# High and low parts of transposed weight operands, side by side instead of one after the other

## The chip, the core and the metric

The kernel runs on one core of a Trainium2 chip. The metric is the device time of one execution in microseconds. Before the change it is 2574.55 us, the median of three runs (2573.84 to 2575.4).

## What is computed

A decoder trunk of two layers on 256 tokens of width 2048, in float32. Each layer has one input projection for four groups of heads (retention, stick-breaking attention, a gated linear recurrence, sparse attention), an output projection, cross-attention into 256 memory tokens, and a gated feed-forward part of width 5632 with a causal convolution of width 3. Cut to the products that matter here:

```
for layer in range(DEPTH):
    proj = rms_norm(x, mix_norm[layer]) @ w_in[layer]
    ...
    mix = jnp.concatenate([o.reshape(B, S, GROUP_WIDTH) for o in (o_ret, o_sb, o_hg, o_nsa)], axis=-1)
    x = x + mix @ w_out[layer]
    x = x + cross_attention(...)            # ends in (o @ wo)
    x = x + conv_ffn(...)                   # ends in (silu(gate) * val) @ w_down
return rms_norm(x, final_norm)
```

## The kernel before, in words

Every float32 matrix product is made of products of parts. A float32 operand v is split into a high part, rounded to the type that the rows call fp32r, and a low part, v minus the high part, of the same type. A product is hi x hi + hi x lo + lo x hi.

The weight matrices come from HBM in **units** of up to 128 x 1024 numbers, in an order fixed by `plan()`. TensorE (PE) multiplies; for each unit SyncE (SP) issues a DMA into `raw`, ScalarE (ACT) writes the high part `hi` (L422), and VectorE (DVE) writes the low part `lo` (L250, called by `u_lo`). These run some units ahead of PE (`AHEAD`, `HI`, `LO`). There are two kinds of units:

- `group_b` (L506, L509): the result is wanted transposed, with features on the partitions. The unit's `hi` and `lo` are the stationary operand (the weights that a load puts into the array) and the activations `xt` stream past: 512 columns at L506 (high and low part of 256 tokens in one go), 256 at L509.
- `group_a` (`mm_a`, L437 to L439): the result is wanted with tokens on the partitions. Here the transposed activations are the stationary operand, 128 tokens at a time, and the unit's `hi` and `lo` stream past, mostly 512 columns. For each block of 128 features and each half of the tokens there are three matmuls: high part against `hi` (L437), high part against `lo` (L438), low part against `hi` (L439). `group_tail` (L473 to L475) does the same for the last chunk of the last down projection, with the second half of the tokens in two pieces of 256 columns each.

In the rows a matmul's operands read out<-moving,stationary, in alphabetical order: acc<-hi,mg at L437 streams `hi` past `mg`.

The transposed activations are tiles of 128 partitions x 2 x 256: high part of 256 tokens, then low part. They have two tags with 16 buffers each. Tiles named `xt` come from the norms; the input projection and the up projection use them on both sides. Tiles named `mg` are, first, the results of the four mixers (made in `to_mix`, `stick`, and `item` in `nsa`), of cross-attention (`xout`) and of the gated feed-forward part (`ev_up`), which are only ever weights, in the output projection, `xattn_wo` and the down projection; and second, the normed memory tokens, which are used on both sides, at L506 and L509 among others and, as weights, for products of 256 columns at L437 to L439. The helper `hi_part` writes the high part on ACT (L245 or L263), `lo_part` the low part on DVE (L250 or L253), from the value and the high part just written.

A weight load is an instruction of its own on PE (PEld in the rows); PE runs it while the matmul before it is still streaming. The order of instructions on each engine is that in which the program is written out: a loop over the units with generators (`tick`) that put the other work between them. Each engine works in its order, and semaphores hold it where operands aren't ready.

Of the kernel before, what the change touches and what calls it, by code (L numbers as in the profile page):

```python
# [10 lines left out]
F32R = mybir.dt.float32r  # L11
# [183 lines left out]
def body(ctx, tc, w, x, xt_in, mem, mem_t, pos, consts, masks, pars, wck, wcv, fnorm, out):  # L195
    nc = tc.nc
    AHEAD, HI, LO = 6, 3, 2
    off, _, _ = shape_consts()
# [3 lines left out]
    flow = ctx.enter_context(tc.tile_pool(name="flow", bufs=1))  # L202
# [7 lines left out]
    def nm(p):  # L210
        count[0] += 1
        return f"{p}{count[0]}"
# [12 lines left out]

    def xt_tile(tag):
        return flow.tile([128, 2, 256], F32R, name=nm(tag), tag=tag, bufs=16)

    def f(ap):
        return ap.bitcast(F32)  # L230
# [443 lines left out]
    def layer(l):  # L674
# [118 lines left out]
        def to_mix(y, heads, base, gname):  # L793

            ps = yield from bank([128, 2, 256])
            for q in range(2):
                for t in range(2):
                    T.transpose(ps[:, q, t * 128:(t + 1) * 128], y[:, t, q, :], ident)
            yield
            o = [xt_tile("mg") for _ in range(2)]  # L800
            for q in range(2):
                hi_part(o[q], ps[:, q, :], pc(l, gname, heads[q]))
            yield
            for q in range(2):
                lo_part(o[q], ps[:, q, :], pc(l, gname, heads[q]))
                mix[base + heads[q]] = o[q]
            drop()
# [158 lines left out]
        def stick(h):  # L966
            yield from need("sq", "sk")
            qh, kh = W["sq"][h // 2][:, h % 2, :], W["sk"][h // 2][:, h % 2, :]
            ps = yield from bank([128, 3, 128])
            pf = ps.rearrange("p a b -> p (a b)")  # L970
            T.matmul(pf[:, 0:256], lhsT=kh[:, 0:128], rhs=qh, start=True, stop=True)
            T.matmul(pf[:, 256:384], lhsT=kh[:, 128:256], rhs=qh[:, 128:256], start=True, stop=True)
            if h == H - 1:
                W.pop("sq")
                W.pop("sk")
            qh = kh = None
            yield
            z, e = s_tile([128, 3, 128]), s_tile([128, 3, 128])
            A.copy(z[:, 1, :], ps[:, 1, :])
            tt(z[:, 0::2, :], ps[:, 0::2, :], bc(c("sbm"), 2), OP.add)  # L980
            drop()
            yield
            act(e, z, AF.Abs)
            act(e, e, AF.Exp, scale=-1.0)
            act(e, e, AF.Ln, bias=1.0)
            yield
            stt(e, z, 0.0, e, OP.max, OP.add)
            yield
            ef = e.rearrange("p a b -> p (a b)")
            ps = yield from bank([128, 384])  # L990
            T.matmul(ps[:, 0:256], lhsT=c("tri"), rhs=ef[:, 0:256], start=True, stop=False)
            T.matmul(ps[:, 128:256], lhsT=c("ones"), rhs=ef[:, 256:384], start=False, stop=False)
            T.matmul(ps[:, 256:384], lhsT=c("tri"), rhs=ef[:, 256:384], start=False, stop=True)
            e = ef = None
            yield
            zf = z.rearrange("p a b -> p (a b)")
            tt(zf, zf, ps, OP.subtract)
            drop()
            yield
            act(zf, zf, AF.Exp)  # L1000
            yield
            yield from need("sv")
            v = W["sv"]
            po = yield from bank([128, 256])
            T.matmul(po, lhsT=v[0][:, cols(h)], rhs=zf[:, 0:256], start=True, stop=False)
            T.matmul(po[:, 128:256], lhsT=v[1][:, cols(h)], rhs=zf[:, 256:384], start=False, stop=True)
            z = zf = v = None
            if h == H - 1:
                W.pop("sv")
            yield  # L1010
            o = xt_tile("mg")
            hi_part(o, po)
            yield
            lo_part(o, po)
            drop()
            mix[4 + h] = o


        def nsa():
            yield from need("nq")  # L1020
            qT = []
            for p in range(2):
                o = yield from to_feat(W["nq"], (2 * p, 2 * p + 1))
# [18 lines left out]
            for i, pn in enumerate(("pk", "pv")):  # L1042
                wn = s_tile([128, 32, 15])
                a = kv[:, i, :].rearrange("p (a b) -> p b a", b=16)
                for u in range(2):
                    o = PC[pn] + 16 * u
# [76 lines left out]
            def item(h, t):  # L1123
                wd = 128 * (t + 1)
                ps = yield from bank([128, 2, wd])
                T.matmul(ps, lhsT=qT[h // 2][:, h % 2, t * 128:(t + 1) * 128], rhs=kT[:, :, 0:wd],
                         start=True, stop=True)
                yield
                p = s_tile([128, 2, wd])
                stt(p, ps, SCALE, bc(c("cm", 256 - wd, 256), 2), OP.mult, OP.add)  # L1130
                drop()
                mx, sm, cf = small(2), small(2), small(2)
                V.tensor_reduce(mx, p, axis=AX.X, op=OP.max)
                ts(mx, mx, -1.0, None, OP.mult)
                yield
                for b in range(2):
                    act(p[:, b, :], p[:, b, :], AF.Exp, bias=mx[:, b:b + 1], accum=sm[:, b:b + 1])
                yield
                ts(sm, sm, 1e-30, None, OP.max)
                V.reciprocal(cf, sm)  # L1140
                tt(cf, cf, gate[t][:, 3 * h + 1:3 * h + 3], OP.mult)
                for b in range(2):
                    ts(p[:, b, :], p[:, b, :], cf[:, b:b + 1], None, OP.mult)
                yield
                ps = yield from bank([128, 2, t + 1, 128])
                for b in range(2):
                    for k in range(t + 1):
                        T.transpose(ps[:, b, k, :], p[:, b, k * 128:(k + 1) * 128], ident)
                p = None
                yield  # L1150
                pT = s_tile([128, 2, t + 1, 128])
                A.copy(pT, ps)
                drop()
                yield
                if t == 0:
                    pos_[h] = yield from bank([128, 256])
                po = pos_[h]
                o = po[:, t * 128:(t + 1) * 128]
                T.matmul(o, lhsT=vc[0:15, :], rhs=pcT[t][0:15, h, :], start=t == 0, stop=False)
                for b in range(2):  # L1160
                    for k in range(t + 1):
                        T.matmul(o, lhsT=nv[:, k, b, :], rhs=pT[:, b, k, :], start=False,
                                 stop=t == 1 and b == 1 and k == t)
                pT = None
                if t == 1:
                    yield
                    o = xt_tile("mg")
                    hi_part(o, pos_[h])
                    yield
                    lo_part(o, pos_.pop(h))  # L1170
                    drop()
                    mix[12 + h] = o
# [216 lines left out]
        def xout(h):  # L1389
            while h not in X["p"]:  # L1390
                yield
            po = yield from bank([128, 256])
            for m in range(2):
                T.matmul(po, lhsT=X["v"][h // 2][:, m, (h % 2) * 128:(h % 2 + 1) * 128], rhs=X["p"][h][:, m, :],
                         start=m == 0, stop=m == 1)
            X["p"][h] = None
            yield
            o = xt_tile("mg")
            hi_part(o, po)
            yield  # L1400
            lo_part(o, po)
            drop()
            xo[h] = o
# [18 lines left out]
        def ev_up(g):  # L1422
            def ev(ps):
                u = yield from whole(ps)
                yield from known(nf)
                tt(u, u, bc(nf.rb, 2), OP.mult)
                yield
                o = s_tile([128, 2, 256])
                for q in range(2):
                    ft = q * FT + g  # L1430
                    act(o[:, q, :], u[:, q, :], AF.Identity, scale=pc(l, "cw", 4 * FT + ft), bias=pc(l, "cb", ft))
                yield
                for q in range(2):
                    ft = q * FT + g
                    stt(o[:, q, 1:256], u[:, q, 0:255], pc(l, "cw", 2 * FT + ft), o[:, q, 1:256], OP.mult, OP.add)
                    stt(o[:, q, 2:256], u[:, q, 0:254], pc(l, "cw", ft), o[:, q, 2:256], OP.mult, OP.add)
                yield
                act(o[:, 0, :], o[:, 0, :], AF.Silu)
                yield
                tt(o[:, 0, :], o[:, 0, :], o[:, 1, :], OP.mult)  # L1440
                yield
                x_ = xt_tile("mg")
                hi_part(x_, o[:, 0, :])
                yield
                lo_part(x_, o[:, 0, :])
                gts[g] = x_
            return ev
# [247 lines left out]
```

## Time and profile before

| | |
|---|---|
| median of 3 runs | 2574.55 us (2573.84 to 2575.4) |
| the profiled execution, its own time | 2574.59 us |
| its span, first to last instruction | 2572.8 us |
| PE busy | 99% |
| PEld busy (weight loads, beside PE) | 85% |
| DVE busy | 69% |
| ACT busy | 53% |
| granted TensorE clock, mean | 0.999 of full |

Busy time of PE is counted from the start of a matmul to its end, and matmuls overlap, so its share is close to 100% wherever they follow without a gap. What a matmul costs in a row of them is read from the distance of two starts. The span is shorter than the execution by what lies ahead of the first instruction and behind the last.

### The profile page before, as it was taken

Reading aid. Unit: us, or ns where it says so; the run is one execution under the profiler, and the core shown is the slowest. Engines: PE = TensorE matmul, PEld = TensorE weight load, DVE = VectorE, ACT = ScalarE, POOL = GpSimd, SP = SyncE. Lnnn points to the kernel's source line nnn. Section 1 sums busy time; section 2 is a strip of 40 time slices with the busy share of each in tenths; the row PEclk is TensorE's granted clock in tenths of the full one; section 3 lists DMA queues with packets and bytes.
Section 4 is the critical chain, followed back from the end, with each engine's and each line's share of the span. In section 5 each row is a group of like instructions: output and inputs, shape, how many; then the busy total and the mean of one; then the engine's idle time right before and its main releaser. Section 6 shows DMA issues by size and latency. Waiting matters only on the chain. (4 is left out here: it accounts for less than half of the span.)

```text
span 2572.8 us, 37308 instructions
## 1 busy us (share of the span) xinstructions
PE 2554.7 (99%) x13866; PEld 2197.5 (85%) x13866; DVE 1777.8 (69%) x2881; ACT 1364.3 (53%) x2158; POOL 45.4 (2%) x79
## 2 busy tenths in 40 slices
PE   9999999999999999999999999999999999999998
PEld 7888888888888888888889888889888888888887
DVE  7776666667767676676767666656686777766766
ACT  6545545565555555455555455445664545454554
POOL 0010000000000000000000100000000000000000
PEclk9999999999999999999999999999999999999999
DMA  8574466545556555556555744655455555556654
GB/s 286 174 231 140 151 202 221 185 149 191 195 190 196 189 195 190 193 187 195 188 183 161 228 134 155 204 182 185 154 193 192 192 192 193 192 190 193 210 190 147
DMA packets 136582, 483.66 MB, mean 188 GB/s; under 512 B 15952, under 2 KB 16464, under 8 KB 136400
## 3 DMA queue, kind: packets, MB, share of 16 engines
q1 hardware_dynamic: 131024, 464.75, 55.0%
q0 software_dynamic: 4800, 15.73, 1.9%
q8 instruction: 109, 1.79, 0.3%
q10 hardware_dynamic: 576, 0.79, 0.1%
q14 instruction: 73, 0.60, 0.1%
HBM read 479.12 MB, written 2.10 MB: 187 GB/s over the span
## 5 line engine op out<-in xcount | busy, mean ns | idle before, releaser
L250 DVE TENSOR_TENSOR lo<-raw,hi 128x1024 fp32r<-128x1024 f32 (+3 forms) x881 | 1066.8, 1212 | 723.8 <-PE acc L438 255.7
L422 ACT CAST hi<-raw 128x1024 fp32r<-128x1024 f32 (+2 forms) x879 | 916.7, 1044 | 1132.1 <-PE acc L439 486.1
L506 PE MATMUL acc<-xt,hi 128*128 128x512 f32 x3456 | 868.8, 394 | 6.1 <-ACT hi L1599 6.1
L506 PEld LDWEIGHTS acc<-xt,hi 128*128 128x128 f32 x3456 | 619.7, 188 | 118.1 <-ACT hi L1599 6.1
L509 PEld LDWEIGHTS acc<-xt,lo 128*128 128x128 f32 x3456 | 460.0, 188 | 36.9
L509 PE MATMUL acc<-xt,lo 128*128 128x256 f32 x3456 | 465.7, 277 | 0.0
L437 PE MATMUL acc<-hi,mg 128*128 128x512 f32 (+1 forms) x1136 | 433.2, 381 | 0.2
L439 PE MATMUL acc<-hi,mg 128*128 128x512 f32 (+1 forms) x1136 | 428.8, 377 | 0.0
L438 PE MATMUL acc<-lo,mg 128*128 128x512 f32 (+1 forms) x1136 | 428.6, 377 | 0.0
L437 PE MATMUL acc<-hi,xt 128*128 128x512 f32 (+2 forms) x640 | 252.1, 394 | 0.0
L439 PEld LDWEIGHTS acc<-hi,mg 128*128 128x128 f32 x1136 | 213.7, 188 | 39.9 <-DVE mg L250 0.3
L437 PEld LDWEIGHTS acc<-hi,mg 128*128 128x128 f32 x1136 | 213.8, 188 | 39.4 <-ACT mg L263 1.0
L438 PEld LDWEIGHTS acc<-lo,mg 128*128 128x128 f32 x1136 | 213.8, 188 | 38.4
L439 PE MATMUL acc<-hi,xt 128*128 128x512 f32 (+2 forms) x640 | 243.1, 380 | 0.0
L438 PE MATMUL acc<-lo,xt 128*128 128x512 f32 (+2 forms) x640 | 242.9, 379 | 0.0
L253 DVE SCALAR_TENSOR_TENSOR s<-s,par,s 128x255 f32<-128x255 f32 x352 | 161.9, 481 | 6.3
L438 PEld LDWEIGHTS acc<-lo,xt 128*128 128x128 f32 x640 | 120.4, 188 | 20.8 <-issue 1.9
L437 PEld LDWEIGHTS acc<-hi,xt 128*128 128x128 f32 x640 | 120.3, 188 | 20.9 <-issue 2.3
L439 PEld LDWEIGHTS acc<-hi,xt 128*128 128x128 f32 x640 | 120.1, 188 | 20.6
L245 ACT ACTIVATE s<-s,par 128x256 f32<-128x256 f32 x176 | 96.1, 594 | 0.4 <-DVE s L250 0.4
L250 DVE TENSOR_TENSOR s<-acc,s 128x256 f32<-128x256 f32 x224 | 83.8, 416 | 0.3 <-ACT s L520 0.3
L250 DVE TENSOR_TENSOR x<-x,acc 128x512 f32<-128x512 f32 x128 | 81.5, 677 | 1.5 <-PE acc L475 1.5
(202 smaller groups left out, 1420.1 us busy)
## 6 DMA issues: line engine op xcount, KB each, us to landing
raw<-in_w_dram SPq DMA_DIRECT2D x847, 512.0 KB, 3.4
raw<-in_w_dram SPq DMA_DIRECT2D x16, 396.0 KB, 3.1
raw<-in_w_dram SPq DMA_DIRECT2D x16, 384.0 KB, 3.0
s<-in_nsa_w_ck_dram POOLq DMA_DIRECT2D x16, 256.0 KB, 5.5
s<-in_nsa_w_cv_dram POOLq DMA_DIRECT2D x16, 256.0 KB, 4.6
s<-in_memt_dram POOLq DMA_DIRECT2D x16, 256.0 KB, 5.3
s<-in_xt_dram SPq DMA_DIRECT2D x8, 256.0 KB, 6.5
x<-in_x_dram SPq DMA_DIRECT2D x8, 256.0 KB, 7.6
```

The costliest lines, as they stand in the source:

```text
L245: A.activation(o, i, func, bias=bias, scale=scale)
L250: V.tensor_tensor(o, a, b, op=op)
L253: V.scalar_tensor_tensor(o, a, s, b, op0=op0, op1=op1)
L422: A.copy(u.hi[:, a:b], u.raw[:, a:b])
L437: T.matmul(ps[t][:, 0:n], lhsT=xh, rhs=hi, start=first, stop=False)
L438: T.matmul(ps[t][:, 0:n], lhsT=xh, rhs=lo, start=False, stop=False)
L439: T.matmul(ps[t][:, 0:n], lhsT=xl, rhs=hi, start=False, stop=last)
L506: T.matmul(st["ps"][q].rearrange("p a b -> p (a b)"), lhsT=u.hi[:, at:at + 128], rhs=xk[kk].rearrange("p a b -> p (a b)"), start=i == 0 an ...
L509: T.matmul(st["ps"][q][:, 1, :], lhsT=u.lo[:, at:at + 128], rhs=xk[kk][:, 0, :], start=False, stop=i == 3 and kk == 3)
```

## The change

A second helper beside `xt_tile` makes a tile of the same size and tag in which the high and the low part of each element lie side by side: 128 partitions x 256 x 2. It gives back a view with the two axes swapped, so that the code which indexes the tile stays as it is: `o[:, 0, :]` is the high part, now with a step of two elements, and `o[:, 1, :]` the low part. The five places which make tiles that serve only as weights call it. The memory tiles, also tagged `mg`, and all `xt` tiles keep the old layout. The order of the instructions on each engine is what it was. Line numbers behind L229 grow by five.

```diff
+    def paired():
+
+        o = flow.tile([128, 256, 2], F32R, name=nm("mg"), tag="mg", bufs=16)
+        return o.rearrange("p a b -> p b a")
+
...
-            o = [xt_tile("mg") for _ in range(2)]
+            o = [paired() for _ in range(2)]
             for q in range(2):
                 hi_part(o[q], ps[:, q, :], pc(l, gname, heads[q]))
...
-            o = xt_tile("mg")
+            o = paired()
             hi_part(o, po)
             yield
             lo_part(o, po)
...
-                    o = xt_tile("mg")
+                    o = paired()
                     hi_part(o, pos_[h])
...
-            o = xt_tile("mg")
+            o = paired()
             hi_part(o, po)
...
-                x_ = xt_tile("mg")
+                x_ = paired()
                 hi_part(x_, o[:, 0, :])
```

## Rows read from the trace of the kernel before

**Rows 1.** The page's first part: busy time, share of the span, instructions.

```profile
PE 2554.7 (99%) x13866; PEld 2197.5 (85%) x13866; DVE 1777.8 (69%) x2881; ACT 1364.3 (53%) x2158; POOL 45.4 (2%) x79
```

**Rows 2.** Waits of PE: who for whom, us in total, times, longest us.

```profile
PE acc L506 <- ACT hi L1599: 6.1, 1, 6.1
PE wk L1394 <- ACT s L1383: 1.3, 2, 0.7
...
```

**Rows 3.** Busy time by stretch, down projection: stretch, us, engines, clock, DMA share, GB/s.

```profile
680.00:710.00 30.00, 30.00 (x134) 24.86 (x133) 19.72 (x25) 12.35 (x14) 0.00 (x0) 1.00 0.59 197
```

**Rows 4.** Timeline of PE in that stretch: start us, length us, what.

```profile
689.92 0.39 PE L439 MATMUL acc<-hi,mg 128*128 128x512 f32 x1
...
690.60 0.39 PE L439 MATMUL acc<-hi,mg 128*128 128x512 f32 x1
```

**Rows 5.** Timeline of PE at the kernel's end, matmuls of 256 columns.

```profile
2560.16 0.28 PE L473 MATMUL acc<-hi,mg 128*128 128x256 f32 x1
...
2560.64 0.28 PE L474 MATMUL acc<-lo,mg 128*128 128x256 f32 x1
```

**Rows 6.** Timeline of PE around a pause after a group.

```profile
1496.40 0.39 PE L438 MATMUL acc<-lo,xt 128*128 128x512 f32 x1
1496.63 0.39 PE L439 MATMUL acc<-hi,xt 128*128 128x512 f32 x1
1497.52 0.60 PE L1114 MATMUL wk<-cst,s 128*15 128x128 f32 x4 [0.50 <-DVE s L250]
```

**Rows 7.** Timeline of the weight loads (PEld) in the same stretch.

```profile
1496.41 0.19 PEld L439 LDWEIGHTS acc<-hi,xt 128*128 128x128 f32 x1
1497.49 0.34 PEld L1114 LDWEIGHTS wk<-cst,s 128*15 128x15 f32 x4 [0.90 <-ACT s L245]
```

**Rows 8.** Timeline of PE where it waited for the last mg tile.

```profile
2536.84 0.39 PE L439 MATMUL acc<-hi,mg 128*128 128x512 f32 x1
2537.31 0.50 PE L437 MATMUL acc<-hi,mg 128*128 128x512 f32 x1
2537.65 0.40 PE L438 MATMUL acc<-lo,mg 128*128 128x512 f32 x1
```

**Rows 9.** Groups by line and form: count, busy us, mean ns, idle before.

```profile
L437 PE MATMUL acc<-hi,mg 128*128 128x512 f32 x1008 | 395.3, 392 | 0.2
L437 PEld LDWEIGHTS acc<-hi,mg 128*128 128x128 f32 x1136 | 213.8, 188 | 39.4 <-ACT mg L263 1.0
L473 PE MATMUL acc<-hi,mg 128*128 128x512 f32 x8 | 3.1, 392 | 0.0
L473 PE MATMUL acc<-hi,mg 128*128 128x256 f32 x8 | 2.3, 282 | 0.0
```

**Rows 10.** Timeline of DVE at the start of `decays`.

```profile
76.47 0.28 DVE L844 COPY s<-s 128x256 f32<-128x256 f32 x1
76.78 0.42 DVE L250 TENSOR_TENSOR s<-s 128x256 f32<-128x256 f32 x1
```

**Rows 11.** Groups by line and form: writers of mg tiles, and one other on ACT.

```profile
L263 ACT CAST mg<-s 128x256 fp32r<-128x256 f32 x88 | 35.0, 398 | 0.0
L263 ACT CAST mg<-wk 128x256 fp32r<-128x256 f32 x24 | 8.5, 369 | 3.7 <-PE wk L1394 2.6 <-PE wk L1162 1.1
L245 ACT ACTIVATE mg<-wk,par 128x256 fp32r<-128x256 f32 x16 | 6.7, 466 | 0.0
L245 ACT ACTIVATE de<-s 128x256 f32<-128x256 f32 x32 | 11.6, 409 | 1.6 <-DVE s L250 1.5
L250 DVE TENSOR_TENSOR mg<-s,mg 128x256 fp32r<-128x256 f32 x88 | 36.9, 419 | 0.7 <-ACT mg L263 0.7
```

**Rows 12.** Timeline of PE in the up projection, merged rows.

```profile
1001.33 1.07 PE L509 MATMUL acc<-xt,lo 128*128 128x256 f32 x8
1002.24 2.00 PE L506 MATMUL acc<-xt,hi 128*128 128x512 f32 x8
1004.08 1.07 PE L509 MATMUL acc<-xt,lo 128*128 128x256 f32 x8
```

## The prediction

> **What bounds the kernel now.** I read the shares of the engines first. TensorE (PE) is busy 2554.7 of 2572.8 us; VectorE (DVE) has 69%, ScalarE (ACT) 53% [rows 1]. Then I asked what PE waits for: the view of waits has five rows for it, the longest 6.1 us before the first matmul, the next 1.3, so at most 6.1 + 4 x 1.3 = 11 us [rows 2]. A stretch of the down projection, 680 to 710 us, shows the same from close by: PE busy 30.00 of 30.00 us at a granted clock of 1.00, weight loads (PEld) 24.86, DVE 19.72, ACT 12.35 [rows 3]. So only what changes the beat of the matmuls changes the time; work on ACT and DVE has cover.
>
> The length that a row gives for a matmul (0.39 us) is not its beat, since matmuls overlap. The beat is the distance of their starts. In the down projection it is 690.60 - 689.92 = 0.68 us for three, 0.227 each for 512 columns [rows 4]. At the end of the kernel the same three lines run with 256 columns: 2560.64 - 2560.16 = 0.48 us for four, 0.120 each [rows 5]. The difference, 0.107 us for 256 columns, is 2.4 columns per ns, the upper clock level. So a matmul of this kind costs columns / 2.4 GHz plus a **fixed part**: 0.227 - 0.213 = 0.0135 us, and 0.120 - 0.107 = 0.0133. That fixed part is the only thing in these stretches that a different weight layout could give back, and the question is what it is.
>
> The rows say that it is not the next weight load disturbing the running matmul. At 1496.63 an L439 matmul of 512 columns starts and takes 0.39 us; the next weight load starts only at 1497.49, when it is over [rows 6, 7]. The matmuls before it take the same 0.39 with a load beside them. A load that reads SBUF in another way can't save what is there without any load. The load itself is short: where PE had waited for the mg tile, the matmul's length includes its own load, 0.50 instead of 0.39, so 0.11 us [rows 8], against a beat of 0.227.
>
> **The change part by part.** No instruction is added, removed or moved; the order on PE, DVE and ACT is the same, waits included, and so are the sizes of all buffers. What changes are steps: 8 bytes instead of 4 between elements of the tiles that `paired` makes, in the reads of weight loads, in the writes of the high part (ACT), and in the read and writes of the low part (DVE).
>
> *Weight loads, 512 columns.* L437, L438 and L439 have 1008 matmuls of 512 columns each with mg weights, and lines 473 to 475 have 8 each in the last chunk (for each of the two trios one row is shown) [rows 9]. Together 3 x 1016 = 3048, and 3048 x 0.227 = 691 us of the time. Each load (0.11 us) lies under the matmul before it (0.227) and has 0.117 us to spare. No row shows a weight load with a step, so its cost is bounded from both sides. From below: 0, by the same step in another reader: the DVE copy at L844 and the addition behind it read and write with step two, and the addition takes 0.42 us [rows 10], as the unstepped mg<-s,mg does (419 ns) [rows 11]. From above: twice the time, 0.22 us, which is still under 0.227. I take 0, since at both ends the load stays covered. A gain is excluded as far as the gain would come from less disturbance, by the matmul at 1496.63.
>
> *Weight loads, 256 columns.* The narrow matmuls of the last chunk, 3 lines x 8 into either of two accumulators (one of these six groups is shown) [rows 9], are 48, with a beat of 0.120 us [rows 5], and 0.11 of load under it; 0 as it is, and with a doubled load 48 x (0.22 - 0.12) = +5 us, all of it on the path, since it is the end of the kernel.
>
> *ACT and DVE.* 128 high parts and 128 low parts are written with the step: 88 + 24 + 16 on ACT, and as many on DVE, which follows each of them [rows 11]. By L844 and its neighbour a step of two costs DVE nothing. For ACT no row writes with a step of two; the nearest writes short runs (de<-s, 409 ns), like other 128x256 forms (398 for mg<-s) [rows 11]. I take 0. If each ACT write cost 0.4 us more, that would be 51 us spread over an engine that is 47% idle; exposed would be the places where PE waits for mg, about 0.24 us at 2537.31 [rows 8] and a few more of that size, at most 2 us in all.
>
> Sum: 0 on 2574.59 us, which is the profiled execution's own time (its span of 2572.8 plus 1.8 around it) and 0.04 above the median of the runs, 2574.55. Forecast: **2574.6 us**. With the bounds (2 us on ACT, 5 us at the end, some us of jitter where weights switch from one unit to the next) its own range is 2570 to 2580.
>
> The weighing against a rule. The fixed part in rows is 0.0135 us. The Trainium skill, "TensorE: Matmul & The Clock Gate", section "Back-to-back issue gap", gives columns / 2.4 + 2.5 ns for a lone stream, so 0.216 us for 512 columns, an estimate of 11 ns below the beat here; the trace doesn't agree, since it shows 0.227 in every undisturbed stretch. By that rule 3048 x 0.011 = 33 us could be there to win, 2541 us.
>
> **The rivals.**
>
> *Faster: the fixed part depends on how the weights lie.* For it speaks one row: L509, with 256 columns, other tiles and other addresses, runs 8 matmuls from 1001.33 to 1002.24, 0.114 each [rows 12]. Its fixed part is 0.114 - 0.107 = 0.007 us, half of the 0.0133 at the end of the kernel. Whatever the cause, the fixed part is no constant of the machine. If a step of two brought the mg matmuls to L509's, 3096 x 0.0066 = 20 us, so **2554 us**; if all of it went, 3096 x 0.0134 = 41 us, 2533, which is the floor. Against it speaks the matmul without a load beside it, and that L506, from the same stretch with the same kind of tiles as L509, has no less than the mg matmuls: 1004.08 - 1002.24 = 1.84 us for 8, 0.230 each.
>
> *Slower: the weight load takes the beat.* A load with a step touches twice the bytes, 1024 instead of 512 per partition. If a load then takes twice as long, 0.22 us, there are only 7 ns left to the 0.227 of a matmul; if it doubles with its fixed part, as the narrow beat would (2 x 0.120 = 0.240), the load sets the beat: 3048 x 0.013 = 40 us and 48 x 0.12 = 6 us, 2620. It decides from the point where load and fixed part pass 0.227. A milder form is a load that now does disturb the stream: L506 stands at 0.230, 3 ns above, and 3 ns on 3048 is 9 us, 2584. Between them I take **2600 us**. For it: the cover is 7 ns if the load doubles. Against it: step two cost DVE nothing.
>
> The Trainium skill, "SBUF — State Buffer", section "Door 1: The DMA port swizzle", says that a reader needs two hits in each 16-byte line for full rate; four-byte elements at a step of eight bytes give just two. By that rule the load keeps its time and the sum stays 0; no row shows it for TensorE.
>
> *The change does nothing to the loads* is not open: the built program's weight operands do step by two.
>
> **How the numbers follow.** Forecast (the beat stays): 0.43. Faster rival: 0.25, because L509 shows that the fixed part can be smaller and nothing here names its cause. Slower rival: 0.32, because the only price that no row bounds well is that of the stepped load. The range reaches from 2550 (the faster rival at L509's price, with a little beyond; some 0.08 is left out) to 2605 (the slower rival up to its middle price and a little more; some 0.09 is left out). Faster by over 0.2% (5.1 us, about what a measurement of this kernel can tell from no change) 0.25, within 0.43, slower 0.32.
>
> **What would show it.** In the profile after: the distance of starts of L442 to L444 (old 437 to 439) in the down projection stays 0.227 if I am right, falls toward 0.220 for the faster rival, rises to 0.230 to 0.240 for the slower. The weight load's own mean (188 ns [rows 9]) stays if the step is free, and grows by about 0.11 us if the load doubles. The narrow matmuls at the end stay at 0.120, or go to about 0.22: they are the most sensitive place, since there the load has no cover. ACT's mg<-s stays at 398 ns and DVE's mg<-s,mg at 419 if step-two writes are free. L506 and L509, which are untouched, must stay at 0.230 and 0.114; if they move, the cause lies outside of all I have argued. The forecast is wrong if the fixed part of 0.0135 us has to do with how the own weights lie in SBUF.

## The result, and the profile after

The changed kernel takes 2594.22 us (median), the kernel before 2574.98 in the same comparison: a ratio of 1.0075, 95% interval 1.0062 to 1.0089. It is slower by some 19 us. That lies in the predicted range, but the likeliest case, no change, did not come about.

The shares of the engines (busy time, share of the span, instructions), as in [rows 1]:

```profile
PE 2574.2 (99%) x13866; PEld 2214.2 (85%) x13866; DVE 1779.5 (69%) x2881; ACT 1367.3 (53%) x2158; POOL 45.6 (2%) x79
```

PE is busy 19.5 us longer with the same 13866 matmuls. Its waits, as in [rows 2] (who for whom, us in total, times, longest), have not grown:

```profile
PE acc L511 <- ACT hi L1604: 6.0, 1, 6.0
PE wk L1399 <- ACT s L1388: 1.3, 2, 0.7
```

So the matmuls themselves take longer. In the stretch of [rows 3] (us, then busy time and count of PE, PEld, DVE, ACT, POOL, then clock) PE is again busy throughout at the full clock, with 130 matmuls in 30 us instead of 134:

```profile
680.00:710.00 30.00, 30.00 (x130) 24.84 (x129) 19.30 (x25) 13.55 (x16) 0.00 (x0) 1.00 0.57 189
```

The beat, as in [rows 4] (start, length, what). These two starts are nine matmuls apart: 2.10 / 9 = **0.233 us**, where it was 0.227:

```profile
689.75 0.39 PE L442 MATMUL acc<-hi,mg 128*128 128x512 f32 x1
...
691.85 0.39 PE L442 MATMUL acc<-hi,mg 128*128 128x512 f32 x1
```

The narrow matmuls at the end, as in [rows 5], keep theirs: 2580.38 - 2579.90 = 0.48 for four, 0.120 each.

```profile
2579.90 0.28 PE L478 MATMUL acc<-hi,mg 128*128 128x256 f32 x1
...
2580.38 0.28 PE L479 MATMUL acc<-lo,mg 128*128 128x256 f32 x1
```

The untouched feature products, as in [rows 12], keep theirs too: (1006.56, 1008.39, 1009.31) 1.83 / 8 = 0.229 and 0.92 / 8 = 0.115.

```profile
1006.56 2.00 PE L511 MATMUL acc<-xt,hi 128*128 128x512 f32 x8
1008.39 1.07 PE L514 MATMUL acc<-xt,lo 128*128 128x256 f32 x8
1009.31 2.00 PE L511 MATMUL acc<-xt,hi 128*128 128x512 f32 x8
```

The groups by line and form, to be held against [rows 9, 11] (after the bar: busy us, mean ns of one, idle time before):

```profile
L442 PE MATMUL acc<-hi,mg 128*128 128x512 f32 x1008 | 400.3, 397 | 0.1
L442 PEld LDWEIGHTS acc<-hi,mg 128*128 128x128 f32 x1136 | 219.4, 193 | 40.2 <-ACT mg L268 1.0
...
L268 ACT CAST mg<-s 128x256 fp32r<-128x256 f32 x88 | 37.1, 421 | 0.0
L255 DVE TENSOR_TENSOR mg<-s,mg 128x256 fp32r<-128x256 f32 x88 | 37.0, 420 | 0.7 <-ACT mg L268 0.7
...
L268 ACT CAST mg<-wk 128x256 fp32r<-128x256 f32 x24 | 8.8, 386 | 3.6 <-PE wk L1399 2.6 <-PE wk L1167 0.8
L250 ACT ACTIVATE mg<-wk,par 128x256 fp32r<-128x256 f32 x16 | 6.9, 484 | 0.0
```

The weight load went from 188 to 193 ns, the matmul from 392 to 397. ACT's writes cost 17 to 23 ns more each, DVE's 1 to 3. Held matmul by matmul against before, the distances of the starts grow by 19.8 us in all, and 19.0 of that stands behind the wide matmuls with stepped weights: 3048 x 6.2 ns.

The matmul without a load beside it, on which the prediction had leaned, changed as well. PE and PEld around a wait for a mg tile, after:

```profile
1267.33 0.39 PE L443 MATMUL acc<-lo,mg 128*128 128x512 f32 x1
1267.56 0.40 PE L444 MATMUL acc<-hi,mg 128*128 128x512 f32 x1
1268.01 0.51 PE L442 MATMUL acc<-hi,mg 128*128 128x512 f32 x1
```
```profile
1267.33 0.19 PEld L444 LDWEIGHTS acc<-hi,mg 128*128 128x128 f32 x1
1268.01 0.20 PEld L442 LDWEIGHTS acc<-hi,mg 128*128 128x128 f32 x1 [0.49 <-ACT mg L268]
```

The same place before:

```profile
1258.11 0.39 PE L439 MATMUL acc<-hi,mg 128*128 128x512 f32 x1
1258.59 0.50 PE L437 MATMUL acc<-hi,mg 128*128 128x512 f32 x1
```

The matmul at 1267.56 ends at 1267.96, before the next load starts (1268.01). It takes 0.40 us (397 ns in the trace's finer count), its counterpart at 1258.11 took 0.39 (388 ns). No load runs while it does. That does not clear the loads: the load of its own weights (1267.33) ran beside the matmul before it, and the next section has a matmul that is longer by what went before it. The ends of matmuls in the profile are modelled, besides, so a single length is weaker evidence than distances of starts.

### The profile page after: what moved, and what is told of

Read it like the earlier page. It is cut to its first block, busy times and chain, and to the rows that moved or that the text cites. A ratio compares the mean times of both kernels' runs of the same rounds, so it can differ in the third digit from the quotient of the medians.

```text
span 2592.6 us, 37308 instructions
## 1 busy us (share of the span) xinstructions
PE 2574.2 (99%) x13866; PEld 2214.2 (85%) x13866; DVE 1779.5 (69%) x2881; ACT 1367.3 (53%) x2158; POOL 45.6 (2%) x79
## 5 line engine op out<-in xcount | busy, mean ns | idle before, releaser
L442 PE MATMUL acc<-hi,mg 128*128 128x512 f32 (+1 forms) x1136 | 438.1, 386 | 0.1
L444 PE MATMUL acc<-hi,mg 128*128 128x512 f32 (+1 forms) x1136 | 433.6, 382 | 0.0
L444 PEld LDWEIGHTS acc<-hi,mg 128*128 128x128 f32 x1136 | 219.2, 193 | 40.7
L442 PEld LDWEIGHTS acc<-hi,mg 128*128 128x128 f32 x1136 | 219.4, 193 | 40.2 <-ACT mg L268 1.0
L443 PEld LDWEIGHTS acc<-lo,mg 128*128 128x128 f32 x1136 | 219.3, 193 | 38.9
```

What stands on the lines that cost most here:

```text
L442: T.matmul(ps[t][:, 0:n], lhsT=xh, rhs=hi, start=first, stop=False)
L443: T.matmul(ps[t][:, 0:n], lhsT=xh, rhs=lo, start=False, stop=False)
L444: T.matmul(ps[t][:, 0:n], lhsT=xl, rhs=hi, start=False, stop=last)
```

## The experiments

Three questions: is the price in the reads, the load's length or the writes; is it the step at all; and what of a tile's place counts. "mg" are the tiles in the sixteen buffers of that tag: the change steps all but the memory tiles among them, an offset moves them all. "Beat" is the mean distance from a matmul's start to the next, over all pairs of the same kind that are under 0.26 us apart.

### Half of the blocks stepped

```diff
+    def paired(k):
+        if k % 2 == 0:
+            return xt_tile("mg")
```
(with the number of the feature block given to it at its five calls)

> The change on odd feature blocks alone (1548 of 3096 matmuls); even blocks keep high part, then low part. Every theory expects about half of the 19.6 us: 2585 us. They part where the layout switches, in the last matmul of a block (low part, second half of the tokens) in the down projection. Theory OWN (a matmul is longer because its own weights were loaded with a step): last matmul of an even block 0.227 us to the next start, last of an odd block 0.233. Theory BESIDE (a matmul is longer because the load that runs beside it steps): the other way round, last of an even block 0.233, last of an odd block 0.227.

Measured: 2586.36 us, ratio 1.0045 (1.0028 to 1.0062), 60% of the change's cost. Within one kernel both beats stand side by side. Timeline of PE, a block with stepped weights and then one with contiguous ones: 0.70 / 3 = 0.233 and 0.68 / 3 = 0.227.

```profile
680.93 0.39 PE L445 MATMUL acc<-lo,mg 128*128 128x512 f32 x1
...
681.63 0.39 PE L445 MATMUL acc<-lo,mg 128*128 128x512 f32 x1
```
```profile
690.63 0.39 PE L445 MATMUL acc<-lo,mg 128*128 128x512 f32 x1
...
691.31 0.39 PE L445 MATMUL acc<-lo,mg 128*128 128x512 f32 x1
```

Where blocks meet, a matmul with contiguous weights beside a stepped load has 0.2304, one with stepped weights beside a contiguous load 0.2325. Neither the own weights nor the load beside carry the price alone. Nor do the two together: the first matmul after a stepped block whose own weights and whose neighbour's are contiguous still has 0.2310, and only those behind it 0.227. Part of the price is handed on from one matmul to the next, which both theories missed.

The same shows where no load runs beside. At the kernel's end a matmul of a contiguous block follows stepped ones (PE, then PEld):

```profile
2570.36 0.40 PE L480 MATMUL acc<-hi,mg 128*128 128x512 f32 x1
```
```profile
2570.14 0.19 PEld L480 LDWEIGHTS acc<-hi,mg 128*128 128x128 f32 x1
2570.87 0.19 PEld L481 LDWEIGHTS acc<-lo,mg 128*128 128x128 f32 x1 [0.55 <-DVE lo L257]
```

It takes 397 ns, as in the changed kernel, though its own load is a contiguous one (187 ns) and the next comes only after it; before the change its length was 388. Two others in this kernel, which pause behind contiguous matmuls, have 388.

### A step of four

```diff
-        o = flow.tile([128, 256, 2], F32R, name=nm("mg"), tag="mg", bufs=16)
+        o = flow.tile([128, 128, 4], F32R, name=nm("mg"), tag="mg", bufs=16)
```
(both halves of the rows and both parts side by side, so that a load takes every fourth element)

> Tiles of 128 x 4: high and low part of both halves of the tokens side by side, so that a load takes every fourth element (16 bytes apart, each in a 16-byte line of its own; 128 lines in 2 KB in place of 64 in 1 KB and 32 in 512 bytes). Theory LINES (the price goes with the lines or bytes that a load passes): with +6.3 ns for +32 lines, +96 lines give +19 ns, a beat of 0.246 us, 3048 x 0.019 = 58 us, 2633 us; narrow matmuls at the end up from 0.120. Theory STEP (any step costs the same): a beat of 0.233 us, 2594 us. Theory BOUND (the load's own time becomes the bound): a beat well over 0.25 us and narrow ones the same as wide ones.

Measured: 2609.63 us, ratio 1.0137 (1.0122 to 1.0152). Here the load does grow, from 193 to 296 ns, and the narrow matmuls at the end, which have no cover, go from 0.120 to (2585.56 - 2584.62) / 4 = 0.235 us:

```profile
L456 PEld LDWEIGHTS acc<-hi,mg 128*128 128x128 f32 x1136 | 336.6, 296 | 1.5 <-ACT mg L282 1.2
```
```profile
2584.62 0.40 PE L493 MATMUL acc<-lo,mg 128*128 128x256 f32 x1
...
2585.56 0.40 PE L494 MATMUL acc<-hi,mg 128*128 128x256 f32 x1
```

The wide beat is 0.235 on the mean, mostly in values from 0.231 to 0.240. So this is what a load that sets the narrow beat looks like, and the change's load (193 ns, narrow beat 0.120) is not one. That wide and narrow now have the same beat is what theory BOUND said, though not at its "well over 0.25". A price in proportion to the bytes that the load spans is not what the wide beat shows: from a step of two to one of four it rises by only 2 ns. Some 5 of the 34 us that the starts grow by are the 47 narrow matmuls, 24 the wide ones in a row (8 ns each), and 5 some forty single wide ones that grow by about 0.12 us each.

The Trainium skill, "SBUF — State Buffer", section "Door 1: The DMA port swizzle", has a reader at full rate with two hits in each 16-byte line. The loads agree: contiguous 188 ns, two hits (step two) 193, one hit (step four) 296. Of the beat with a covered load the section says nothing.

### No step, another place

Two kernels without any step. In the first the mg tiles of the kernel before lie 64 bytes further in each partition:

```diff
+    flow.tile([128, 16], F32, name="edge3", tag="edge3")
```

> The kernel before with all mg tiles 64 bytes further on in SBUF (the place that lo tiles have as weights at L509), no step. Theory PLACE (the fixed part of 0.0135 us depends on where weights lie, as L509's smaller 0.007 suggests): a beat of 0.220 us in the down projection, narrow matmuls 0.114, about 20 us less, 2555 us. Theory NO PLACE: 0.227 and 0.120, 2574.6 us.

In the second the weights of the feature products (hi at 192 bytes, lo at 64, modulo 256) are put to 0:

```diff
-        at = 16 if u.by_feature else 0
+        at = 0
...
-        at = 48 if u.by_feature else 0
+        at = 0
```

> The kernel before with the weights of group_b (hi, lo) at the start of their buffers in place of 192 and 64 bytes behind it. Theory PLACE: L509's fixed part goes from 0.007 to 0.013 us, 3584 x 0.006 = 22 us more, 2596 us, and L506 changes as well. Theory NO PLACE: L509 stays at 0.114 us, L506 at 0.230, 2574.6 us.

Measured: 2594.18 us, ratio 1.0077 (1.0062 to 1.0092), and 2594.28, ratio 1.0077 (1.0062 to 1.0092). Moving contiguous weights by 64 bytes costs as much as the whole change, with the weight load at its old 188 ns. Groups and PE's timeline of the first; 2.10 / 9 = 0.233:

```profile
L437 PEld LDWEIGHTS acc<-hi,mg 128*128 128x128 f32 x1136 | 213.6, 188 | 45.1 <-ACT mg L263 1.0
```
```profile
689.72 0.40 PE L437 MATMUL acc<-hi,mg 128*128 128x512 f32 x1
...
691.82 0.39 PE L437 MATMUL acc<-hi,mg 128*128 128x512 f32 x1
```

In the second it is the narrow feature products (L509) that pay: 0.95 / 8 = 0.119 instead of 0.114, 17 us on 3456 of them. The wide ones in these rows stay at 1.84 / 8 = 0.230; over all 3456 they grow by 0.6 ns each, 2 us.

```profile
1005.93 1.12 PE L509 MATMUL acc<-xt,lo 128*128 128x256 f32 x8
1006.88 2.00 PE L506 MATMUL acc<-xt,hi 128*128 128x512 f32 x8
1008.72 1.11 PE L509 MATMUL acc<-xt,lo 128*128 128x256 f32 x8
```

So the beat depends on where the weights lie, and 64 bytes that are bad for a wide matmul are good for a narrow one: in the first kernel the narrow mg beat fell from 0.120 to 0.115.

### Place by itself, or distance from the moving operand

First both are moved by 64 bytes, the mg tiles and the hi and lo tiles that stream past them; then these hi and lo tiles alone:

```diff
-        at = 16 if u.by_feature else 0
+        at = 16
...
-        at = 48 if u.by_feature else 0
+        at = 48 if u.by_feature else 16
...
+    flow.tile([128, 16], F32, name="edge3", tag="edge3")
```
(the last line only in the first of the two)

> The kernel before with its contiguous transposed tiles; the sixteen mg tiles and also the moving operands of the row products (their hi and lo tiles) lie 64 bytes further in each partition. offset64, which moved the mg tiles alone, took 2594.2 us. Theory RELATIVE (what counts is the distance of the weights from the moving operand): the 3048 wide mg products are back at 0.227 us and the narrow ones at 0.120, while the 1536 wide products on xt tiles, which stay where they were, come to a distance of -64 bytes and gain up to 3 ns each (the beat that the feature products had at that distance), 5 us at most: 2575 to 2580 us. Theory ABSOLUTE (the place of the weights by itself counts): wide mg products at 0.233 us as in offset64, 2594 us.

> The kernel before; only the moving operands of the row products (hi and lo tiles) lie 64 bytes further, the mg and xt tiles stay. Theory RELATIVE: 3048 + 1536 wide products at a distance of -64 bytes, about 0.230 us instead of 0.227, some 14 us: 2588 us. Theory ABSOLUTE: the weights have not moved, 2574.6 us.

Measured: 2580.05 us, ratio 1.0021 (1.0011 to 1.0030), and 2582.95, ratio 1.0031 (1.0019 to 1.0043). With both moved, the mg products are back at 2.04 / 9 = 0.227 us:

```profile
689.64 0.39 PE L437 MATMUL acc<-hi,mg 128*128 128x512 f32 x1
...
691.68 0.39 PE L437 MATMUL acc<-hi,mg 128*128 128x512 f32 x1
```

The place by itself is out: it foretold 2594 for the first and no change for the second. Of the two theories the distance holds. Of the 5.2 us by which the starts of the first still grow, 2.2 are the 1536 wide products on xt, now 64 bytes off the other way (1.5 ns each). Another 1.4 are other products whose distance changed: 0.9 where the memory tiles, moved as well, stream past (L506, L509), 0.5 at 396 columns on xt. The rest is mainly 1.1 and 0.8 us on the feature products on xt, which were not moved, without a cause that I can name. In the second the products on mg and xt grew by 0.9 to 2.2 ns, foretold as 3, so its 14 us came out as 8.

The two kernels also bear on [rows 6, 7]. The L439 matmul on xt that ends a group, with no load beside it, is this one when the moving operand lies 64 bytes off (PE, then PEld):

```profile
1499.74 0.40 PE L439 MATMUL acc<-hi,xt 128*128 128x512 f32 x1
```
```profile
1499.52 0.19 PEld L439 LDWEIGHTS acc<-hi,xt 128*128 128x128 f32 x1
1500.57 0.09 PEld L1114 LDWEIGHTS wk<-cst,s 128*15 128x15 f32 x1 [0.87 <-ACT s L245]
```

397 ns, where [rows 6] has 388 in the finer count: the same 9 ns as in the changed kernel, and again with no load running. Here no load steps at all.

### Step and place together, and the writes alone

The changed kernel with its mg tiles 64 bytes further (the one line of "edge3" above):

> The changed kernel (weights at every other element) with the sixteen mg tiles 64 bytes further. If the step's price is one of its own and the place's another, they add: 0.239 us a beat, 38 us, 2612 us. If both are one effect (where the weights that are read stand against the moving operand, and every other element leaves the place partly wrong whatever the offset), the beat stays about 0.233 us, 2594 us; if the place undoes what the step did, 0.227 us and 2575 us.

The writers as in the changed kernel, the loads over 128 contiguous elements of the same tile:

```diff
+            self.w = o.rearrange("p a b -> p b a")
+            self.r = o.rearrange("p a b -> p (a b)").rearrange("p (b a) -> p b a", b=2)
```

> The writers (ScalarE and VectorE) put the halves at every other element as in the changed kernel; the weight loads read 128 contiguous elements of the same tile, so the weight operands are other elements than the reference's in this kernel. Theory READS (all of the price is in loading weights at every other element): ScalarE's casts stay at the changed kernel's 0.421 us, the wide beat is 0.227 us, 2574.6 to 2577 us. Theory WRITES (the later writers, or what the matrix engine meets while they write, make the price): 0.233 us, 2594 us.

Measured: 2585.14 us, ratio 1.0041 (1.0027 to 1.0055), and 2576.01, ratio 1.0004 (0.9995 to 1.0013). The second settles where the price is. ACT keeps its longer writes, the matmul its old length, and the time is that of before:

```profile
L450 PE MATMUL acc<-hi,mg 128*128 128x512 f32 x1008 | 395.3, 392 | 1.1 <-DVE mg L263 1.1
...
L276 ACT CAST mg<-s 128x256 fp32r<-128x256 f32 x88 | 36.9, 419 | 0.0
```

The first says that step and place don't add (that was 2612): 64 bytes, which cost contiguous weights 19.6 us, give stepped ones 9 back. Its beat is 2.07 / 9 = 0.230:

```profile
689.81 0.39 PE L442 MATMUL acc<-hi,mg 128*128 128x512 f32 x1
...
691.88 0.39 PE L442 MATMUL acc<-hi,mg 128*128 128x512 f32 x1
```

In this kernel the matmul before the wait for a mg tile, with no load beside it (the next starts at 1263.11), is as short as before the change, 387 ns, although the beat is 0.231:

```profile
1262.64 0.39 PE L444 MATMUL acc<-hi,mg 128*128 128x512 f32 x1
```
```profile
1263.11 0.19 PEld L442 LDWEIGHTS acc<-hi,mg 128*128 128x128 f32 x1 [0.51 <-ACT mg L268]
```

So the length of such a matmul does not follow the beat, and can't stand for it.

### The other distances

The same "edge3" with 32 or 48 elements instead of 16 in the kernel before and in the changed one, and `at = 32` instead of 48 for the hi tiles of the feature products:

> The kernel before with its contiguous tiles; the sixteen mg tiles lie 128 bytes further, their moving operands stay. At a distance of 0 the wide beat was 0.227 us and the narrow one 0.120, at 64 bytes 0.233 and 0.115, at -64 bytes (moving64) 0.229 and 0.117. Theory PERIOD (the distance counts in steps of 128 bytes): 0.227 and 0.120, 2574.6 us. Theory DISTANCE (the further the later): 0.233 us or more on 3048 products, 2594 us or more, 2 us back on the narrow ones.

> The changed kernel with its mg tiles 128 bytes further. At 0 the stepped wide beat was 0.2333 us (2594 us), at 64 bytes 0.2308 (2585 us). Theory OWN PRICE (a step of two costs some 4 ns a product whatever the place): 0.231 us, 2585 us at best. Theory PLACE (at some distance the step costs nothing): 0.227 us here or at 192 bytes, 2575 us.

> The changed kernel with its mg tiles 192 bytes further. Theory OWN PRICE: 0.231 us, 2585 us at best. Theory PLACE: 0.227 us here or at 128 bytes, 2575 us.

> The kernel before; the hi tiles of the feature products (weights of 3456 wide products with moving xt or mg) lie 128 bytes from the moving operand instead of 192, so nothing of the step is in it. At 192 these products had a beat of 0.229 us, at 0 (weights_at_zero) 0.2305, with floors of 0.2267 seen elsewhere. If 128 bytes is their best place: up to 8 us less, 2566 us. If the place matters only as hit or miss of one distance: 0.229 to 0.233 us, 2574 to 2590 us.

Measured: 2592.44 us (ratio 1.0068, 1.0053 to 1.0083), 2590.61 (1.0060, 1.0045 to 1.0075), 2594.55 (1.0076, 1.0061 to 1.0091) and 2588.22 (1.0052, 1.0035 to 1.0068). None is a better place than that of the kernel before. All beats in one table, in us; the distance is the weights' address less the moving operand's, modulo 256 bytes. The profile has no addresses; the distances are worked out from the sizes and the order of the tiles in the kernels:

| distance | 512 columns, contiguous | 512 columns, stepped | 256 columns, contiguous |
|---|---|---|---|
| 0 | 0.2270 (before, mg); 0.2305 (weights_at_zero, hi) | 0.2334 (the change) | 0.120 (before, mg); 0.119 (weights_at_zero, lo) |
| 64 | 0.2333 (offset64) | 0.2308 (step2_at64) | 0.115 (offset64, mg); 0.114 (before, lo) |
| 128 | 0.2324 (offset128); 0.2321 (hi_at128) | 0.2315 (step2_at128) | 0.119 (offset128, mg) |
| 192 | 0.2290 (moving64); 0.2286 (before, hi) | 0.2333 (step2_at192) | 0.117 (moving64, mg) |

Tiles of quite different use (mg, xt, hi, lo) agree at equal distance within 0.001 us, but for the wide hi tiles at 0, which are 3.5 ns above mg. The memory tiles are a test from the other side, since as moving operand they moved under weights that stayed: their wide beats fit the table (offset64, distance 128: 0.2324; offset128, distance 64: 0.2329), their narrow one at 0 does not (offset64: 0.117). So the distance explains most of the beat, not all. Stepped weights reach 0.227 at no place that was tried; their best is 0.231, which is 10 us slower than before.

## Why the prediction was right or wrong

*What bounds the kernel.* Right: PE is busy throughout, its waits stayed, and the whole loss is beat times count.

*Weight loads, 512 columns: the step that failed.* The term was taken at 0 "since at both ends the load stays covered". The load did stay covered (193 ns against 188, and the narrow beat still 0.120), and yet the term measured +19.0 us. The error lies one step earlier, in the reading of the matmul at 1496.63 [rows 6, 7]: as it was as long without a load beside it, I took it that a load's way of reading SBUF can't enter the beat. What that row shows is less: that the *next* load isn't needed for that length. The length depends on the layout all the same, seen on that very matmul when its moving operand was shifted (397 instead of 388 ns); it can be handed on by the matmuls before it (397 ns at 2570.36 in the half-stepped kernel); and it need not follow the beat (387 ns at a beat of 0.231). So it could settle nothing about the beat. That the fixed part has to do with how the own weights lie is what the prediction named as making it wrong.

*The fixed part.* I took 0.0135 us as one part, common to 512 and 256 columns, since 0.227 and 0.120 gave the same remainder. That was a chance meeting of places (L506 and L509, at others, have 0.229 and 0.1145): at a distance of 0 wide matmuls are at the lowest beat seen (0.227) and narrow ones well above theirs (0.114).

*The faster rival.* Its premise, that the fixed part depends on how the weights lie, is what the runs showed, and L509's 0.114 [rows 12] does come from its place: put to a distance of 0, it has 0.119. Its sign was wrong: wide matmuls on mg already had the best of the places tried, and the step led away from its beat.

*The slower rival.* Right in sign, and its milder price (3 ns on 3048) is half of what came (6.2 ns). Its dearer price, 2620 us for a load that doubles and takes the beat, is not at work in the change (188 to 193 ns); step4 shows such a load at work, in the narrow matmuls. The 2600 us between the two is what stretched the range to 2605, so that the time lies in it is luck as far as the forecast's own mechanism goes. Its milder form, a load that does disturb the stream, is not excluded: where layouts meet, a stepped load beside a contiguous matmul raises its beat by 3 ns, and the lengths without a load beside can't speak against it.

*Narrow matmuls, ACT, DVE.* Right. The narrow beat stayed at 0.120; DVE's writes stayed at 420 ns. ACT's step-two writes were not free as I took them (398 to 421 ns), but they are covered, as the bound said: with them alone the kernel stays within 0.13% of before.

*The weighing against a rule.* The lowest mean beats in these kernels are 0.227 us for 512 and 0.114 for 256 columns, 14 and 7 ns above columns / 2.4 GHz; 0.227 is not that of every undisturbed stretch, as the prediction has it, since the wide feature products have 0.229. The Trainium skill, "TensorE: Matmul & The Clock Gate", section "Back-to-back issue gap", has 2.5 ns above it for a lone stream, an estimated 0.216 us for 512 columns. No kernel here came down to that, so the 33 us that the prediction worked out from it were not there to win by a layout that was tried.

*What stays open.* Why the distance of weights and moving operand counts modulo some bytes, why a step of two changes the beat, and what one matmul hands on to the next. That both are read from SBUF at about the same time and get in each other's way would fit, but no run separates that from an effect inside PE. The distances were tried in steps of 64 bytes only.

## What to carry to other kernels

Where TensorE is busy throughout, the beat of its matmuls is worth measuring from the starts, by kind, before and after any change of layout: 6 ns in 227 were 19 us here, and no wait and no load's length explains them. The place of weights against the moving operand in SBUF is a thing to try out (64 bytes more in each partition are all that a shift takes), separately for each width of matmul, since what was best for 512 columns was worst for 256. A row that is unchanged when something is absent shows only that this thing isn't needed for it just then, not that a change of it is free; and a single matmul's length is no substitute for the beat.

## What the runs showed of the hardware that was not expected

- Contiguous weights moved by 64 bytes against the moving operand: wide beat 0.227 to 0.233 us, narrow beat 0.120 to 0.115, with the load at 188 ns in both.
- Weights at every second element: load 188 to 193 ns, wide beat 0.227 to 0.233, narrow beat unchanged at 0.120. At every fourth: load 296 ns, narrow beat 0.235.
- The price is handed on: a matmul with contiguous weights and a contiguous load beside it has a beat of 0.2310 us right behind stepped ones, 0.227 further on.
- ACT writing 128x256 elements with a step of two takes 421 instead of 398 ns, DVE's subtraction 420 instead of 419. With a step of four (step4) they take 655 and 618.
